# Weight splits of the second layer kept in order, a second copy of the mask, and four value cells moved

## The chip, the cores and the metric

The kernel runs on one core of one Trainium2 chip. The metric is the device time of one execution in microseconds, and the time given for a kernel is the median of several executions. The engines are TensorE (PE for its matmuls, PEld for its weight loads), VectorE (DVE), ScalarE (ACT), GpSimd (POOL) and SyncE (SP). Each has its own instruction queue, worked off in order. Transfers are started by an instruction on SP, ACT or POOL and run on the core's DMA engines beside the computing.

## The reference

Two layers over 2048 latent tokens of width 1024, with 256 context tokens in front. Layer 0 is a latent attention beside a gated linear attention. Layer 1, the one that changes here, is a neighbourhood attention of 16 heads of 64:

```python
def odd_mixer(h, hc, w_in, q_gain, k_gain, rpb, w_out, update_ctx):
    def heads(u):
        bsz, n, _ = u.shape
        q, k, v, z = jnp.split(u, 4, axis=-1)
        sh = lambda t: t.reshape(bsz, n, C_HEADS, C_HD)
        return rms_norm(sh(q), q_gain), rms_norm(sh(k), k_gain), sh(v), z

    q_x, k_x, v_x, z_x = heads(jnp.dot(h, w_in))
    q_c, k_c, v_c, z_c = heads(jnp.dot(hc, w_in))
    o = neighborhood_attention(q_x, k_x, v_x, k_c, v_c, rpb)
    y = jnp.dot(o.reshape(h.shape[0], h.shape[1], C_WIDTH) * jax.nn.silu(z_x), w_out)
```

`neighborhood_attention` lets each query see a window of 8 rows by 16 columns of the token grid and all context tokens; a bias table `rpb` is added to the window's scores, and what lies outside the window is masked. All is fp32.

## The kernel before, in words

Matrix products run in split precision: an operand is split into a high and a low part, and a product is three matmuls (lines 129 to 131: high by high, high by low, low by high). A weight is split so: SP loads a raw piece of 128x512 into `wraw`, ACT copies it to the high part, DVE subtracts that from the raw piece to make the low part (lines 380 to 383).

The program goes through layer 0, then the projection of layer 0 (`project`), then three stages of layer 1:

- `odd_qk`, queries and keys. The input weight has eight column blocks j of 512: 0 and 1 make queries, 2 and 3 keys, 4 and 5 values, 6 and 7 gates. A cell (t, j) is the product of token tile t (0 to 17, two of them context) with block j, 24 matmuls into a `gm` tile of PSUM. For queries and keys the cell is normed: ACT squares it, DVE sums (`oss`), POOL takes the power -1/2, and DVE multiplies into `onat` (line 1182). `fin` transposes `onat` on TensorE in a later cell (`tp`, line 1190), ACT and DVE copy the result (`oqh`, `oql`, `okt`), and SP and POOL store it (`Q1`, `K1`, `K1t`). The stage ends with the last two tiles over j = 0, 1, 2, 3 and 6; a gate cell goes through `gate` (line 1242) and is stored to `z1`.
- `odd_vz`, values (stored to `V1`, `V1c` from `ovz` tiles) and gates, woven with `maxes`, which finds a bound on each query's scores. Its zero halves `mz` are cleared by DVE at the stage's start.
- `odd_attention`, head by head: scores `st` from `q1`, `q2` and the keys (lines 1423, 1424), bias tables `tab0`, `tab1` with the mask added by POOL (line 1420), exponentials, products with the values `ov`.

A weight block has one of four places in SBUF (`OD_PLACE`), w0 to w3, so blocks 4, 5, 6 and 7 come into the places of 2, 3, 0 and 1 once those are done with. A generator per block, `od_steps`, makes the splits; `pump` (line 158) advances it at every fourth step of the cells, so the splits lie among the cells' other work on ACT and DVE. The order on each engine is set by a scheduler when the program is built, except where `issue_after` puts one instruction behind another of its engine. The loads of `odd_attention` go through `load` (line 111), which chains them on SP in the order of the code: second query piece of the first heads, keys, values, tables, context keys `kc`, first query piece, and so on, with the mask `maskk` behind them.

Of the kernel before, what the change touches and what calls it, by code (L numbers as in the profile page):

```python
# [10 lines left out]
F32 = mybir.dt.float32  # L11
F32R = mybir.dt.float32r
# [5 lines left out]
P = 128  # L18
# [70 lines left out]
class Kern:  # L89
    def __init__(self, tc, nc, ins, scr):  # L90
        self.tc, self.nc, self.i, self.scr = tc, nc, ins, scr
        self.n = 0
        self.ahead, self.calls, self.chain = [], 0, None

    def pool(self, es, name, bufs=1, space=None, **kw):
        if space is None:
# [100 lines left out]
    def rpow(self, out, in_, mul, add):  # L197

        g = self.nc.gpsimd
        g.tensor_scalar(out=out, in0=in_, scalar1=mul, scalar2=add, op0=ALU.mult, op1=ALU.add)  # L200
        shp = list(out.shape)
        g.tensor_tensor(out=out, in0=out, in1=self.mhalf[:, : shp[1]], op=ALU.pow)


    def consts(self, es):
# [803 lines left out]
    def even_mix(self, e1, win, hT):  # L1009
# [3 lines left out]
        with ExitStack() as es:  # L1013
# [57 lines left out]
            self.prep_pool(e1, "prp1", "left", 2, 3)  # L1071
            ws = [self.pool(e1, "owS", side="left", reuse_waits="tile")]

            def ahead():
# [59 lines left out]

    OD_PLACE = {2: 0, 3: 1, 0: 2, 1: 3, 4: 0, 5: 1, 6: 2, 7: 3}

    def od_steps(self, dst, j, ws):
        n = self.OD_PLACE[j]
        steps = self.split_steps(dst, j, ws[n // 2], self.i["w_od"][:, j], KD, 512, f"w{n}", 1)
        for k, _ in enumerate(steps):  # L1140
            if k % 2:
                yield

    def odd_qk(self, ws, win, hT):
        nc = self.nc
# [6 lines left out]
        with ExitStack() as es:  # L1152
# [5 lines left out]
            self.ahead += [self.od_steps(win, 0, ws), self.od_steps(win, 1, ws)]  # L1158
            pend, kt = [], {}

            def cell(t, j):
                hi, lo = hT[t]
                wh, wl = win[j]
                ps = self.tl(pp, [P, 8, 64], "gm", bufs=3)
                steps = self.mm3_steps(ps[:], (lambda k: hi[:, k, :], lambda k: lo[:, k, :]),
                                       (lambda k: wh[:, k, :], lambda k: wl[:, k, :]), range(KD))
                for n, _ in enumerate(steps):
                    if n == 5 and pend and (len(pend) > 1 or j == 6):
                        fin(*pend.pop(0))
                    yield  # L1170
                if j == 6:
                    n = self.tl(sp, [P, 512], "onat", bufs=4)
                    self.gate(n, ps[:].rearrange("p h d -> p (h d)"))
                    pend.append((t, j, n))
                    return
                sq = self.tl(sp, [P, 512], "osq")
                self.act(sq[:], ps[:].rearrange("p h d -> p (h d)"), AF.Square)
# [4 lines left out]
                nc.vector.tensor_tensor(out=n[:].rearrange("p (h d) -> p h d", h=8), in0=ps[:],  # L1182
                                        in1=ss[:].unsqueeze(2).to_broadcast([P, 8, 64]), op=ALU.mult)
                pend.append((t, j, n))

            def fin(t, j, n):
# [9 lines left out]
                self.act(hi[:], ps[:], AF.Copy, scale=qkg[:, z : z + 1])  # L1196
                j0 = (j % 2) * 4
                if z == 1:
                    nc.sync.dma_start(self.K1[j0 : j0 + 4, :, t * P : t * P + P].rearrange("j p t -> p j t"), hi[:].bitcast(F32))
                if z == 0 or t < NCT:  # L1200
                    lo = self.tl(sp, [P, 4, P], "oql", F32R)
                    nc.vector.scalar_tensor_tensor(out=lo[:], in0=ps[:], scalar=qkg[:, z : z + 1], in1=hi[:],
                                                   op0=ALU.mult, op1=ALU.subtract)
                    if z == 0:
                        for part, tt in enumerate((hi, lo)):
                            nc.sync.dma_start(self.Q1[part][j0 : j0 + 4, :, (t - NCT) * P : (t - NCT) * P + P].rearrange("j p t -> p j t"),
                                              tt[:].bitcast(F32))
                    else:
                        store_k((hi, lo), j0, t * P, P)
                    return  # L1210
                g, r0 = divmod(2 * (t - NCT), 8)
                if r0 == 0:
# [5 lines left out]
                    nc.vector.scalar_tensor_tensor(out=ol, in0=view(ps, 2)[:, :, r], scalar=qkg[:, z : z + 1],  # L1218
                                                   in1=view(hi, 2)[:, :, r], op0=ALU.mult, op1=ALU.subtract)
                if r0 == 6:  # L1220
                    store_k(kt.pop(j), j0, CTX + g * 512, 512)

            def store_k(parts, j0, o, w):

                for u, x in enumerate(parts):
                    for i in range(2):
                        nc.gpsimd.dma_start(self.K1t[j0 : j0 + 4, i, u * 64 : u * 64 + 64, o : o + w].rearrange("j d t -> d j t"),
                                            x[i * 64 : i * 64 + 64].bitcast(F32))

            nxt = {2: 4, 3: 5, 0: 6, 1: 7}  # L1230
            done = lambda j: j in nxt and self.ahead.append(self.od_steps(win, nxt[j], ws))
            cells = self.cells(list(range(NT)), (2, 3, 0, 1), lambda t, j: j > 1 or t >= NCT)[:-8]
            cells += [(t, j) for j in (0, 1, 2, 3, 6) for t in (NT - 2, NT - 1)]
            for _ in self.stream(cells, hT, cell, lambda t: self.prep(1, t, self.x1, pp, ("px", 2)), done):
                self.pump()
            while pend:
                fin(*pend.pop(0))

    def gate(self, out, in_):

# [16 lines left out]
    def odd_vz(self, ws, win, hT):  # L1257
# [3 lines left out]
        with ExitStack() as es:  # L1261
# [6 lines left out]
            def cell(t, j):  # L1268
                hi, lo = hT[t]
                wh, wl = win[j]  # L1270
                ps = self.tl(pp, [P, 512], "gm")
                yield from self.mm3_steps(ps[:], (lambda k: hi[:, k, :], lambda k: lo[:, k, :]),
                                          (lambda k: wh[:, k, :], lambda k: wl[:, k, :]), range(KD))
                n = self.tl(sp, [P, 512], "ovz", bufs=3)
                if j < 6:
                    self.act(n[:], ps[:])
                    self.store_v(t, j - 4, n)
                    return
                self.gate(n, ps[:])
                pt = self.tl(pp, [P, 4, P], "tp", bufs=1)  # L1280
                for i in range(4):
                    nc.tensor.transpose(pt[:, i, :], n[:, i * P : i * P + P], self.ident[:])
# [73 lines left out]
    def odd_attention(self, out, right, left, wout):  # L1356
# [4 lines left out]
        with ExitStack() as es:  # L1361
# [56 lines left out]
            def mask(tabs):  # L1418
                for tb in tabs:
                    nc.gpsimd.tensor_tensor(out=tb[:], in0=tb[:], in1=mk[:], op=ALU.add)  # L1420

            def scores(ps, k1, k2, q1, q2):
                nc.tensor.matmul(ps, k1, q1, start=True, stop=False)  # L1423
# [99 lines left out]
            all_k, most_k = slice(0, KD), slice(0, KD - 1)  # L1523
# [18 lines left out]
            for j in range(8):  # L1542
                OA[j] = {}, {}
                for s, (kind, n) in enumerate(steps):
                    g, c = divmod(n, 4)
                    if j < 7:
# [4 lines left out]
                        elif s == 7:  # L1551
                            Q[j + 1, 1] = query(j + 1, 1)
                        elif s == 13:
                            V[j + 1] = values(j + 1)
                            values_ctx(j + 1, V[j + 1])
                        elif s == 15:
                            kc[j + 1] = keys(j + 1, 0, CTX, kcp, "kc")
                        elif s == 10:
                            with self.tc.issue_after(self.psum.ins):
                                mask(tabs[j + 1])  # L1560
# [200 lines left out]
```

## Time and profile before

| | us |
|---|---|
| median of 3 runs | 3669.73 (3668.54 to 3671.02) |
| profiled execution | 3676.2 |
| its span, first to last instruction | 3674.1 |
| layer 0 | 0 to 1993 |
| projection of layer 0 | 1993 to 2172 |
| queries and keys, `odd_qk` | 2172 to 2626 |
| values and gates, `odd_vz` | 2626 to 3089 |
| `odd_attention` with its projection | 3089 to 3674 |

Times in the trace count from the start of the span. A line number belongs to the kernel whose trace it is. A matmul's duration overlaps the next one's, so that TensorE's rate is read from the starts. In a row of a timeline, what stands in brackets is how long the engine was idle before it and whose end it waited for.

### The profile page before, as it was taken

To read this page: it belongs to the slowest core of one execution; us is meant where nothing else is said; L and a number is where in the kernel's file an instruction comes from. 1 tells how busy PE (TensorE), PEld (TensorE's weight loads), DVE (VectorE), ACT (ScalarE), POOL (GpSimd) and SP (SyncE) were. 2 spreads that over 40 slices of the span, in tenths; PEclk is the share of its full clock that TensorE was granted. 3 is DMA by queue.
4 is the path that set the end of the run, shared out by engine and by line. 5 is a ranking of instruction groups with operands and counts; after the bars stand their busy time and mean duration, and the time that the engine had idled before them with its cause. 6 is when DMAs were issued, how large, how long until landed. Compare 5 with 4: busy or idle time off the path is not lost.

```text
span 3674.1 us, 51831 instructions
## 1 busy us (share of the span) xinstructions
PE 3565.7 (97%) x18404; PEld 2758.7 (75%) x18404; DVE 2363.0 (64%) x4860; ACT 1437.0 (39%) x2741; POOL 1205.6 (33%) x1336
## 2 busy tenths in 40 slices
PE   8999999999999999999999999999899999999998
PEld 6988998888886666655556878888688887555577
DVE  4677666888876666687664444454578784666721
ACT  5545551111125555555553124444422223555510
POOL 1433330101111212122201233333334443777743
PEclk9999999999999999999999999999999999999899
DMA  7455472222241232243622544455744447788554
GB/s 253 145 155 155 133 210 87 80 73 88 75 137 53 83 98 79 85 115 109 177 67 96 188 161 123 141 157 160 227 146 122 146 120 190 210 215 219 175 178 149
DMA packets 364372, 512.19 MB, mean 139 GB/s; under 512 B 25825, under 2 KB 243889, under 8 KB 358210
## 3 DMA queue, kind: packets, MB, share of 16 engines
q1 hardware_dynamic: 322642, 425.49, 39.8%
q0 software_dynamic: 19872, 55.92, 5.1%
q10 hardware_dynamic: 21600, 27.46, 2.1%
q8 instruction: 146, 2.39, 0.3%
q14 instruction: 112, 0.92, 0.1%
HBM read 329.38 MB, written 179.37 MB: 138 GB/s over the span
## 4 chain that ended last, share of the span: by engine, by line
PE 69%; issue 15%; POOL 5%; DVE 5%; DMA 4%; ACT 2%; SPq 0%; POOLq 0%; DVEq 0%; ACTq 0%
PE av L922 7%; PE gm L129 6%; PE gm L130 6%; PE gm L131 6%; PE st L980 4%; PE st L981 4%; PE st L982 4%; PE st L129 2%; PE st L131 2%; PE st L130 2%; PE pj L131 2%; PE pj L130 2%; PE pj L129 2%; PE o L1456 2%; DMA wraw<-w_od 1%
## 5 line engine op out<-in xcount | busy, mean ns | idle before, releaser
L971 DVE TENSOR_TENSOR acc<-acc,apt 128x512 f32<-128x512 f32 x512 | 364.8, 737 | 153.5 <-ACT apt L106 150.6
L106 ACT ACTIVATE apt<-st 128x512 f32<-128x512 f32 (+1 forms) x592 | 344.6, 594 | 290.5 <-PE st L982 257.4
L662 DVE TENSOR_REDUCE mm<-mx 128x1 f32<-128x512 f32 (+1 forms) x656 | 393.2, 630 | 89.9 <-PE mx L661 81.8
L922 PE MATMUL av<-apt,av 128*64 128x512 f32 (+1 forms) x1184 | 286.4, 599 | 0.0
L980 PE MATMUL st<-aq,akh 97*128 97x512 f32 (+1 forms) x592 | 255.7, 432 | 9.7 <-DMA aq<-QT 6.1
L661 PE MATMUL mx<-mk,mq 96*128 96x512 f32 (+1 forms) x656 | 238.6, 372 | 0.0
L981 PE MATMUL st<-aq,akh 96*128 96x512 f32 (+1 forms) x592 | 236.7, 400 | 0.0
L982 PE MATMUL st<-aq,akl 96*128 96x512 f32 (+1 forms) x592 | 235.3, 398 | 0.0
L1330 DVE CUSTOM_DVE_ANT_1 mx<-mx,mtab 128x217 f32<-128x217 f32 (+11 forms) x576 | 184.6, 338 | 49.2 <-PE mx L1324 37.9
L106 ACT ACTIVATE opt<-opt 128x930 f32<-128x930 f32 (+9 forms) x144 | 119.2, 830 | 248.0 <-POOL opt L1627 141.0
L106 ACT ACTIVATE u<-gm 128x352 f32<-128x352 f32 (+1 forms) x144 | 70.5, 496 | 360.4 <-PE gm L131 208.7
L1587 DVE TENSOR_TENSOR opt<-st,tab 128x64 f32<-128x64 f32 (+10 forms) x576 | 142.8, 316 | 88.2 <-PE st L1424 58.1
L922 PEld LDWEIGHTS av<-apt,av 128*64 128x64 f32 x1184 | 81.9, 138 | 156.4 <-issue 154.8
L980 PEld LDWEIGHTS st<-aq,akh 97*128 97x128 f32 x592 | 113.5, 192 | 101.6 <-issue 49.5
L1462 POOL TENSOR_TENSOR oacc<-oacc,opt 128x682 f32<-128x682 f32 (+10 forms) x144 | 169.8, 1199 | 26.4 <-ACT opt L106 25.1
L982 PEld LDWEIGHTS st<-aq,akl 96*128 96x128 f32 x592 | 114.6, 194 | 25.8
L661 PEld LDWEIGHTS mx<-mk,mq 96*128 96x128 f32 x656 | 122.7, 188 | 11.7
L981 PEld LDWEIGHTS st<-aq,akh 96*128 96x128 f32 x592 | 115.3, 195 | 18.3
L1423 PE MATMUL st<-q,kt 128*128 128x480 f32 (+5 forms) x256 | 99.6, 391 | 23.8 <-DVE opt L1587 18.9
L106 ACT ACTIVATE x<-px,modB,modA 128x128 f32<-128x128 f32 x272 | 99.3, 469 | 58.1 <-PE px L331 46.3
L129 PE MATMUL gm<-w0h,hhi 128*128 128x512 f32 x288 | 116.1, 403 | 0.0
L129 PE MATMUL gm<-w1h,hhi 128*128 128x512 f32 x288 | 115.7, 402 | 0.0
(570 smaller groups left out, 9928.1 us busy)
## 6 DMA issues: line engine op xcount, KB each, us to landing
q<-Q SPq DMA_DIRECT2D x48, 512.0 KB
H<-x ACTq DMA_DIRECT2D x36, 512.0 KB
adaw<-ada_w SPq DMA_DIRECT2D x64, 256.0 KB
x<-H SPq DMA_DIRECT2D x32, 512.0 KB
wraw<-w_od SPq DMA_DIRECT2D x64, 256.0 KB
K1t<-okt POOLq DMA_DIRECT2D x32, 512.0 KB, 7.6
kt<-K1t SPq DMA_DIRECT2D x32, 512.0 KB
mtab<-rpb_q SPq DMA_DIRECT2D x16, 899.0 KB
```

What stands on the lines that cost most here:

```text
L106: return self.nc.scalar.activation(out, in_, func, **kw)
L129: self.nc.tensor.matmul(out, lh(k), rh(k), start=j == 0, stop=False)
L130: self.nc.tensor.matmul(out, lh(k), rl(k), start=False, stop=False)
L131: yield self.nc.tensor.matmul(out, ll(k), rh(k), start=False, stop=j == n - 1)
L661: mm = nc.tensor.matmul(ps[:, :w], q[:A_QK, (t % 6) * P : (t % 6) * P + P], k[:A_QK, k0 : k0 + w], start=True, stop=True)
L662: nc.vector.tensor_reduce(out=m[:, t, n : n + 1], in_=ps[:, :w], axis=AX.X, op=ALU.max)
L922: nc.tensor.matmul(O[j, nb][i * 64 : i * 64 + 64, :w], V[j, kt // TT][:, kt % TT, i * 64 : i * 64 + 64], pts[i][:, :w], start=n == 0, stop ...
L971: nc.vector.tensor_tensor(out=acc[i][:, :w], in0=a[:, :w], in1=pts[i][:, :w], op=ALU.add)
L980: nc.tensor.matmul(ps[:, :w], kh[: A_QK + 1, i, kq], qh[: A_QK + 1, :w], start=True, stop=False)
L981: nc.tensor.matmul(ps[:, :w], kh[:A_QK, i, kq], ql[:A_QK, :w], start=False, stop=False)
L982: mm = nc.tensor.matmul(ps[:, :w], kl[:A_QK, i, kq], qh[:A_QK, :w], start=False, stop=True)
L1330: nc.vector.tensor_tensor_reduce(out=s, in0=s, in1=tb[:, ri : ri + rn, ci : ci + cn], scale=1.0, scalar=-3e38, op0=ALU.add, op1=ALU.max, a ...
```

## The change

Five things are changed.

1. `od_steps` makes one stream of all blocks that are to be split (`todo`). The low part is eight tiles of 128x512 instead of one, and the raw piece k is loaded straight into the slot of low tile k + 1; only the last goes through `wraw`, which has two buffers instead of three. Up to four pieces are loaded ahead of their splits in the order of the code.
2. `marks`: in `pump`, the splits are put behind the last cell's square, gate or copy on ACT, and behind its `onat` multiply on DVE.
3. The stores of `K1t` on POOL are issued one at a time, at the second and sixth step of a cell, behind the last power on POOL.
4. The cells (16, 4) and (17, 4), values of the last two tiles, are done at the end of `odd_qk` instead of at the start of `odd_vz`.
5. The mask is loaded twice: a first copy into a free buffer of `q10` directly behind the first heads' tables, for these tables, and a second into `maskk` as before, for the later heads.

```diff
@@ pump
-            if next(self.ahead[0], self) is not self:
+            with ExitStack() as es:
+                for x in self.marks.values():
+                    es.enter_context(self.tc.issue_after(x.ins))
+                r = next(self.ahead[0], self)
+            if r is not self:
                 break
@@ even_mix
-            self.prep_pool(e1, "prp1", "left", 2, 3)
...
-                for j in (2, 3):
-                    yield from self.od_steps(win, j, ws)
+                yield from self.od_steps(win, ws)
@@ od_steps
-    def od_steps(self, dst, j, ws):
-        n = self.OD_PLACE[j]
-        steps = self.split_steps(dst, j, ws[n // 2], self.i["w_od"][:, j], KD, 512, f"w{n}", 1)
-        for k, _ in enumerate(steps):
-            if k % 2:
-                yield
+    def od_steps(self, dst, ws):
+        nc, todo, raw, k = self.nc, self.todo, [], KD
+        def split(w, parts, pool, n, k):
+            hi, lo = parts
+            lo.append(self.tl(pool, [P, 512], f"w{n}l{k}", F32R, bufs=1))
+            self.act(hi[:, k, :], w[:])
+            nc.vector.tensor_tensor(out=lo[k][:], in0=w[:], in1=hi[:, k, :], op=ALU.subtract)
+        while raw or todo or k < KD:
+            for i in range(2):
+                if raw and (len(raw) >= 4 or k == KD and not todo):
+                    split(*raw.pop(0))
+                if k == KD and todo:
+                    j, k = todo.pop(0), 0
+                    n = self.OD_PLACE[j]
+                    pool = ws[n // 2]
+                    dst[j] = self.tl(pool, [P, KD, 512], f"w{n}h", F32R, bufs=1), []
+                if k < KD:
+                    w = self.tl(pool, [P, 512], f"w{n}l{k + 1}", bufs=1) if k < KD - 1 else self.tl(self.prp, [P, 512], "wraw", bufs=2)
+                    nc.sync.dma_start(w[:], self.i["w_od"][:, j, k])
+                    raw.append((w, dst[j], pool, n, k))
+                    k += 1
+            yield
@@ odd_qk
-                    if n == 5 and pend and (len(pend) > 1 or j == 6):
+                    if n == 5 and pend and (len(pend) > 1 or j in (4, 6)):
                         fin(*pend.pop(0))
+                    if n % 4 == 1 and out_k:
+                        with self.tc.issue_after(self.power.ins):
+                            out_k.pop(0)()
                     yield
+                if j == 4:
+                    n = self.tl(sp, [P, 512], "onat", bufs=4)
+                    self.act(n[:], ps[:].rearrange("p h d -> p (h d)"))
+                    self.store_v(t, 0, n)
+                    return
...
-            cells += [(t, j) for j in (0, 1, 2, 3, 6) for t in (NT - 2, NT - 1)]
+            cells += [(t, j) for j in (0, 1, 2, 3, 6, 4) for t in (NT - 2, NT - 1)]
@@ odd_vz
-            cells = [(t, j) for j in (7, 4, 5) for t in (NT - 1, NT - 2)]
+            cells = [(t, j) for j in (7, 5) for t in (NT - 1, NT - 2)]
@@ odd_attention
             tabs[0] = tables(0)
+            first = self.tl(qa, [P, SEQ], "q10", bufs=2)[:, : NR * NC]
+            mask(tabs[0], load_mask(first.rearrange("p (r c) -> p r c", r=NR)))
             kc[0] = keys(0, 0, CTX, kcp, "kc")
...
-            mk = self.tl(ap, [P, NR, NC], "maskk", bufs=1)
-            self.load(mk[:], self.i["maskk"].rearrange("p (r c) -> p r c", r=NR))
-            mask(tabs[0])
+            mk = load_mask(self.tl(ap, [P, NR, NC], "maskk", bufs=1)[:])
```

What this does to the order is shown at three places: first before, then after. At the start of `odd_qk`, SP loads the raw pieces of blocks 0 and 1, places w2 and w3, among the stores of keys:

```order
L380 DMA wraw_4095_19415<-w_od 128x512
L380 DMA wraw_4096_19419<-w_od 128x512
L380 DMA wraw_4107_19476<-w_od 128x512
L1199 DMA K1<-oqh_4093_19400 128x4x128
L380 DMA wraw_4108_19480<-w_od 128x512
L380 DMA wraw_4112_19510<-w_od 128x512
L380 DMA wraw_4113_19514<-w_od 128x512
L380 DMA wraw_4604_22647<-w_od 128x512
L1199 DMA K1<-oqh_4110_19495 128x4x128
```

The same place on SP after the change:

```order
L1163 DMA w3l3_4114_19428<-w_od 128x512
L1163 DMA w3l4_4116_19433<-w_od 128x512
L1163 DMA w3l5_4128_19491<-w_od 128x512
L1163 DMA w3l6_4130_19496<-w_od 128x512
L1163 DMA w3l7_4135_19527<-w_od 128x512
L1238 DMA K1<-oqh_4111_19410 128x4x128
L1163 DMA wraw_4652_22767<-w_od 128x512
L1238 DMA K1<-oqh_4132_19509 128x4x128
```

The pieces come ahead of the first store of keys, each into a slot of its own. At the end of `odd_qk`, DVE's queue before holds the splits of block 5 (`w1l`), then the copies of the last key tile (`okt`), then the multiply of the last key cell, `onat_4670`:

```order
L1179 TENSOR_REDUCE oss_4669_22998<-osq_4668_22996 128x8
L1218 SCALAR_TENSOR_TENSOR okt21_4537_22236<-tp_4664_22966,oqkg_4068_19263,oqh_4665_22971 128x256
L383 TENSOR_TENSOR w1l_4673_23018<-wraw_4674_23019,w1h_4672_23017 128x512
L383 TENSOR_TENSOR w1l_4673_23018<-wraw_4675_23023,w1h_4672_23017 128x512
L383 TENSOR_TENSOR w1l_4673_23018<-wraw_4678_23051,w1h_4672_23017 128x512
L1218 SCALAR_TENSOR_TENSOR okt31_4545_22283<-tp_4676_23033,oqkg_4068_19263,oqh_4677_23038 128x256
L383 TENSOR_TENSOR w1l_4673_23018<-wraw_4679_23055,w1h_4672_23017 128x512
L1218 SCALAR_TENSOR_TENSOR okt31_4545_22283<-tp_4676_23033,oqkg_4068_19263,oqh_4677_23038 128x256
L1182 TENSOR_TENSOR onat_4670_23002<-gm_4661_22939,oss_4669_22998 128x512
L1242 SCALAR_TENSOR_TENSOR onat_4680_23059<-onat_4680_23059,gm_4671_23004 128x512
```

DVE's queue after, where `onat_4715` is the same multiply:

```order
L1218 TENSOR_REDUCE oss_4714_23032<-osq_4713_23030 128x8
L1150 TENSOR_TENSOR w0l2_4709_23020<-w0l3_4696_22957,w0h_4689_22922 128x512
L1150 TENSOR_TENSOR w0l3_4711_23025<-w0l4_4698_22962,w0h_4689_22922 128x512
L1258 SCALAR_TENSOR_TENSOR okt21_4565_22264<-tp_4707_23001,oqkg_4082_19277,oqh_4708_23006 128x256
L1221 TENSOR_TENSOR onat_4715_23036<-gm_4702_22972,oss_4714_23032 128x512
L1150 TENSOR_TENSOR w0l4_4717_23052<-w0l5_4704_22988,w0h_4689_22922 128x512
L1150 TENSOR_TENSOR w0l5_4720_23058<-w0l6_4706_22993,w0h_4689_22922 128x512
L1258 SCALAR_TENSOR_TENSOR okt31_4573_22311<-tp_4722_23069,oqkg_4082_19277,oqh_4723_23074 128x256
L1150 TENSOR_TENSOR w0l6_4724_23088<-w0l7_4710_23023,w0h_4689_22922 128x512
L1287 SCALAR_TENSOR_TENSOR onat_4728_23098<-onat_4728_23098,gm_4716_23038 128x512
L1150 TENSOR_TENSOR w0l7_4726_23093<-wraw_4712_23028,w0h_4689_22922 128x512
L1150 TENSOR_TENSOR w1l0_4730_23115<-w1l1_4719_23056,w1h_4718_23055 128x512
```

The multiply stands ahead of all splits of block 5, which have moved behind the gate cells, and only splits of block 4 (w0) are left around it. Where attention begins, SP's chain of loads before is:

```order
L111 DMA tab0_5482_27513<-rpb_k 128x1034
L111 DMA tab1_5483_27514<-rpb_k 128x1034
L111 DMA kc1_5484_27517<-K1t 128x2x256
L111 DMA kc20_5474_27494<-K1t 64x2x256
L111 DMA q10_5485_27520<-Q1 64x2048 x2
L111 DMA q20_5486_27521<-Q1 64x2048
L111 DMA q20_5486_27521<-M1 1x2048
L111 DMA kt1_5487_27526<-K1t 128x2x512
L111 DMA kt21_5477_27497<-K1t 64x2x512
L111 DMA ov_5481_27511<-V1c 128x2x128
L111 DMA maskk_5488_27530<-maskk 128x1034
```

And after:

```order
L111 DMA tab0_5538_27569<-rpb_k 128x1034
L111 DMA tab1_5539_27570<-rpb_k 128x1034
L111 DMA q10_5540_27573<-maskk 128x1034
L111 DMA kc1_5541_27577<-K1t 128x2x256
L111 DMA kc20_5530_27550<-K1t 64x2x256
L111 DMA q10_5542_27580<-Q1 64x2048 x2
L111 DMA q20_5543_27581<-Q1 64x2048
L111 DMA q20_5543_27581<-M1 1x2048
L111 DMA kt1_5544_27586<-K1t 128x2x512
L111 DMA kt21_5533_27553<-K1t 64x2x512
L111 DMA ov_5537_27567<-V1c 128x2x128
L111 DMA maskk_5545_27590<-maskk 128x1034
```

The mask's first copy, in a `q10` buffer, has come in behind the tables; the rest follows as before. The buffers' places in SBUF have moved as well: with `wraw` one buffer smaller, `tab1` of the first heads takes up a stretch that the last `ovz` tile of `odd_vz` occupied, and its load waits in the program for that tile's store to `V1c` and for ACT's copy into it. Before, this was not so for any load ahead of the second heads' tables.

More of the change, by code (lines that the diff above doesn't have):

```diff
@@ L92, in __init__ @@
         self.n = 0
-        self.ahead, self.calls, self.chain = [], 0, None
+        self.ahead, self.calls, self.chain, self.marks = [], 0, None, {}
     def pool(self, es, name, bufs=1, space=None, **kw):
@@ L201, in rpow @@
         shp = list(out.shape)
-        g.tensor_tensor(out=out, in0=out, in1=self.mhalf[:, : shp[1]], op=ALU.pow)
+        self.power = g.tensor_tensor(out=out, in0=out, in1=self.mhalf[:, : shp[1]], op=ALU.pow)
     def consts(self, es):
@@ L1208, in fin @@
                     else:
-                        store_k((hi, lo), j0, t * P, P)
+                        for f in store_k((hi, lo), j0, t * P, P):
+                            f()
                     return
@@ L1220, in fin, with store @@
                 if r0 == 6:
-                    store_k(kt.pop(j), j0, CTX + g * 512, 512)
+                    out_k.extend(store_k(kt.pop(j), j0, CTX + g * 512, 512))
             def store_k(parts, j0, o, w):
[L1225 to L1228, printed above, removed]
+                def store(u, x, i):
+                    nc.gpsimd.dma_start(self.K1t[j0 : j0 + 4, i, u * 64 : u * 64 + 64, o : o + w].rearrange("j d t -> d j t"),
+                                        x[i * 64 : i * 64 + 64].bitcast(F32))
+                return [lambda u=u, x=x, i=i: store(u, x, i) for u, x in enumerate(parts) for i in range(2)]
             nxt = {2: 4, 3: 5, 0: 6, 1: 7}
-            done = lambda j: j in nxt and self.ahead.append(self.od_steps(win, nxt[j], ws))
+            done = lambda j: j in nxt and self.od_ahead(win, ws, nxt[j])
             cells = self.cells(list(range(NT)), (2, 3, 0, 1), lambda t, j: j > 1 or t >= NCT)[:-8]
-            cells += [(t, j) for j in (0, 1, 2, 3, 6) for t in (NT - 2, NT - 1)]
+            cells += [(t, j) for j in (0, 1, 2, 3, 6, 4) for t in (NT - 2, NT - 1)]
             for _ in self.stream(cells, hT, cell, lambda t: self.prep(1, t, self.x1, pp, ("px", 2)), done):
@@ L1237, in odd_qk @@
                 fin(*pend.pop(0))
+            for f in out_k:
+                f()
+            self.marks = {}
     def gate(self, out, in_):
@@ L1416, in tables, with mask, load_mask @@
                 return tabs
-            def mask(tabs):
+            def mask(tabs, mk):
                 for tb in tabs:
-                    nc.gpsimd.tensor_tensor(out=tb[:], in0=tb[:], in1=mk[:], op=ALU.add)
+                    nc.gpsimd.tensor_tensor(out=tb[:], in0=tb[:], in1=mk, op=ALU.add)
+            def load_mask(mk):
+                self.load(mk, self.i["maskk"].rearrange("p (r c) -> p r c", r=NR))
+                return mk
             def scores(ps, k1, k2, q1, q2):
```

24 lines of the change are left out of this document (15 added, 9 removed).

## The prediction

> **What bounds the kernel now.** I read the page's busy times first, then busy time by stage, then the waits of TensorE in the stages that the change touches, then the two timelines where a wait is long.
>
> ```profile
> PE 3565.7 (97%) x18404; PEld 2758.7 (75%) x18404; DVE 2363.0 (64%) x4860; ACT 1437.0 (39%) x2741; POOL 1205.6 (33%) x1336
> ...
> 1993.00:2172.00 179.00, 177.63 (x787) 146.08 (x786) 70.16 (x75) 32.24 (x50) 45.46 (x36) 1.00 0.55 178
> 2172.00:2626.50 454.50, 438.14 (x2097) 361.10 (x2096) 236.74 (x368) 217.12 (x413) 173.95 (x219) 0.98 0.54 161
> 2626.50:3089.00 462.50, 457.45 (x2227) 382.79 (x2226) 328.31 (x1361) 116.20 (x193) 188.45 (x168) 0.99 0.48 146
> 3089.00:3130.00 41.00, 36.36 (x218) 23.23 (x218) 21.96 (x65) 18.92 (x30) 28.30 (x22) 0.92 0.83 212
> ```
>
> A stage row holds its stretch, its length, busy time of PE, PEld, DVE, ACT and POOL, the granted clock, the DMA share and GB/s. TensorE is the bound. No matmul is added or removed (the four value cells only change stage), so only TensorE's idle time and slowed time can move: 454.50 - 438.14 = 16.4 us idle in queries and keys, 5.0 in values and gates, 4.6 at the start of attention. The waits name them (us in total, times, longest), those of queries and keys first:
>
> ```profile
> PE tp L1190 <- DVE onat L1182: 8.4, 3, 6.7
> PE tp L1190 <- ACT oqh L106: 3.0, 1, 3.0
> PE px L331 <- DVE x L328: 2.9, 1, 2.9
> PE gm L129 <- DVE hhi L343: 1.9, 1, 1.9
> ...
> PE tp L1282 <- DVE ovz L1242: 5.0, 2, 3.1
> PE st L1423 <- DVE opt L1587: 4.2, 2, 3.6
> ```
>
> Idle time is followed by slowed matmuls. In these stretches PE is busy but for the second, and the granted clock (third figure from the end) is half:
>
> ```profile
> 2199.80:2203.20 3.40, 3.31 (x10) 2.71 (x11) 3.15 (x6) 2.33 (x6) 1.35 (x4) 0.50 1.00 318
> 2617.00:2626.50 9.50, 6.28 (x20) 4.79 (x20) 5.60 (x9) 5.78 (x11) 3.67 (x6) 0.50 0.73 199
> 2640.20:2643.60 3.40, 3.40 (x10) 2.63 (x9) 0.00 (x0) 0.70 (x2) 2.40 (x1) 0.51 1.05 394
> 2817.70:2821.10 3.40, 3.40 (x11) 2.91 (x11) 3.37 (x14) 0.51 (x1) 0.00 (x0) 0.51 0.49 188
> 3099.50:3104.40 4.90, 4.90 (x14) 2.42 (x16) 2.90 (x17) 2.77 (x4) 3.18 (x3) 0.50 0.78 238
> ```
>
> Half the busy time is lost there: 1.7, 3.1, 1.7, 1.7 and 2.4 us.
>
> **The end of queries and keys (splits kept in order, value cells as filler).** ACT and DVE in order of time:
>
> ```profile
> 2614.22 0.63 ACT L106 ACTIVATE w1h<-wraw 128x512 fp32r<-128x512 f32 x1 [4.20 <-DMA wraw<-w_od]
> ...
> 2614.88 0.69 DVE L383 TENSOR_TENSOR w1l<-wraw,w1h 128x512 fp32r<-128x512 f32 x1 [4.15 <-ACT w1h L106]
> 2616.00 0.68 DVE L1182 TENSOR_TENSOR onat<-gm,oss 128x512 f32<-128x512 f32 x1
> 2629.89 0.48 DVE L1291 MEMSET mz<- 64x512 f32 x1 [4.67 <-DMA z<-oqh]
> 2637.16 1.03 DVE L1291 MEMSET mz<- 64x512 f32 x2 [6.79 <-DMA z<-oqh]
> ```
>
> The reader is to see a queue: a split whose raw piece has not landed stops ACT, its other half stops DVE, and the `onat` multiply behind it makes TensorE wait 6.7 us. Afterwards DVE waits for the gate store `z<-oqh` before it clears `mz`, so that the `ovz` multiply behind that clearing comes 3.1 us late. The change puts `onat` ahead of the w1 splits and two more cells in front of the stores' readers. A matmul starts every 0.23 us, so a cell of 24 takes 5.5 us (rows of the junction, below). What can go is 8.4 - 0.9 (one of the three waits is at the stage's start) + 3.0 + 3.1 = 13.6 us, with 3.1 + 1.7 of clock: 18.4. I take 15, since the splits, the loads of `maskq`, `mk` and `mq`, and the gate stores still have to land in time in the longer tail.
>
> **The start of queries and keys.** The 2.9 us wait and the 0.9 us behind it come from the same kind of queue:
>
> ```profile
> 2195.93 1.29 DVE L383 TENSOR_TENSOR w3l<-wraw,w3h 128x512 fp32r<-128x512 f32 x2 [2.55 <-ACT w3h L106]
> 2197.14 0.75 DVE L328 TENSOR_SCALAR x<-x,ssx 128x1024 f32<-128x1024 f32 x1
> ```
>
> With raw pieces loaded into eight slots of the weight itself instead of three shared ones, the loads run ahead. 2.9 + 0.9 + 1.7 of clock = 5.5 us; I take 4, since sixteen 256 KB loads then also run against the tiles' own loads.
>
> **Smaller terms.** The 1.9 us wait for `hhi`: 1 us taken. The second `tp <- ovz` wait, 5.0 - 3.1 = 1.9 us with 1.7 of clock at 2817, lies in a stage whose order shifts without a reason to mend it: 0, between -3.6 and +3.6. In the projection 179.00 - 177.63 = 1.4 us is idle: half taken, 0.7. The spread stores of K1t go behind POOL's `pow`; an issue takes some 0.6 us of POOL (four in 2.48 us), but the buffers they read come free later, and they are issued between cells that need `oss`. The row nearest to that is the 3.0 us wait for `oqh`: -2.5 taken, with nothing and -5 as ends. Gains so far 15 + 4 + 1 + 0.7 - 2.5 = 18.2 us.
>
> ```profile
> 2623.64 2.48 POOL L1227 DMA_DIRECT2D K1t<-okt  x4 [0.33 <-ACT okt L106]
> ```
>
> **The junction to attention.** Here the change costs. The last matmuls of values and gates, the last store, and SP's loads (start, us of issue, what):
>
> ```profile
> 3088.27 0.39 PE L130 MATMUL gm<-w1l,hhi 128*128 128x512 f32 x1
> 3088.50 0.39 PE L131 MATMUL gm<-w1h,hlo 128*128 128x512 f32 x1
> 3088.73 0.39 PE L1423 MATMUL st<-q,kc 128*128 128x512 f32 x1
> ...
> 3065.81 1.45 SPq L111 DMA_DIRECT2D tab<-rpb_k  x2
> 3067.35 1.03 SPq L111 DMA_DIRECT2D kc<-K1t  x2
> 3068.43 2.60 SPq L111 DMA_DIRECT2D q<-Q  x3
> ...
> 3089.82 0.54 POOL L1251 DMA_DIRECT2D V1c<-ovz  x1 [2.41 <-ACT ovz L106]
> 3094.50 4.69 POOL L1420 TENSOR_TENSOR tab<-tab,maskk 128x1034 f32<-128x1034 f32 x2 [4.14 <-DMA maskk<-maskk]
> ...
> DMA to landing us min/median/max: 2.3/8.2/10.0
> ```
>
> Before, both tables, `kc` and `q10`/`q20` are issued 20 us ahead of the last matmul (3065.81 against 3088.5), so the scores follow on it at 3088.73; what waits later is the mask, 4.2 us. In the changed program `tab1` of the first heads lies over the buffer of the last `ovz` tile, because `wraw` is one buffer smaller and everything behind it moves down 2 KB. Its load therefore waits until the last `V1c` store has landed, and behind it in SP's queue stand the mask, `kc1`, `kc20`, both `q10`, `q20`, which the first scores read.
>
> Worked out from the last matmul's end G = 3088.9: the store is issued at G + 0.9 and lands 2.3 to 10.0 us later (last row above, of the four such stores), so `tab1` starts at G + 3.2 to G + 10.9. I take the quick end: the slow stores had maskk, q and table loads beside them, and now nothing is ahead of the wait. Sizes on the path:
>
> ```profile
> q<-Q SPq DMA_DIRECT2D x48, 512.0 KB
> tab<-rpb_k SPq DMA_DIRECT2D x16, 517.0 KB
> kc<-K1t SPq DMA_DIRECT2D x8, 256.0 KB
> kc<-K1t SPq DMA_DIRECT2D x8, 128.0 KB
> maskk<-maskk SPq DMA_DIRECT2D x1, 517.0 KB
> ...
> 3093.00:3099.50 6.50, 2.26 (x9) 1.28 (x8) 3.74 (x10) 0.44 (x1) 4.69 (x2) 0.85 0.92 229
> ```
>
> Table, mask, keys and three query pieces are 517 + 517 + 256 + 128 + 3 x 512 = 2954 KB = 3.02 MB: 13.2 us at the 229 GB/s of this stage, 7.7 us at the 394 GB/s above, the fastest stretch shown. I take 229, since its transfers are of the same kinds. Six matmuls (1.4 us) need no `q20` and run while it comes. So the scores lose 3.2 + 13.2 - 1.4 = 15.0 us, and the old wait of 4.2 falls away: net 10.8 us worse. Both quick: 5.3. Slow store: 10.9 + 13.2 - 1.4 - 4.2 = 18.5. The slowed stretch behind the stall is there before and after.
>
> [...]
>
> **Sum.** -18.2 + 10.8 = -7.4 us. The profiled execution took 3676.2 us (span 3674.1, 2.1 outside it), so 3668.8 for it. The median of the runs, 3669.73, stands 6.5 lower; the same difference gives 3662.3.
>
> Three gaps of 2.9, 3.1 and 1.9 us are each followed by a half-clock row above (2199.8, 2640.2, 2817.7). [...]
>
> **The rivals.**
> - The junction is cheap. The store lands in 2.3 us, the loads run at 394 GB/s, and the scores' first loads prove to be elsewhere than I place them, so that it costs from 0 to 5.3 us: -18.2 + 0 to 5.3, so 3651.5 to 3657. For it: SP's queue is empty but for these loads. Against it: `q` rows are long pieces on 64 partitions, in the 229 GB/s stage.
> - The junction is dear. The last store lands after 10.0 us, as the slowest did: -18.2 + 18.5 = +0.3, 3670. For it: the median landing, 8.2 us, is nearer to this end. Against it: a busier DMA then.
> - Slower: the wait at the end of queries and keys moves and does not go. The w1 splits still stand in ACT's queue ahead of the copy of the last gate tile and of the values; eight pieces of 256 KB, 2.1 MB, must land within the two cells (11 us) before they are due, 191 GB/s. Below that rate ACT stops again, the gate store leaves late, and `mz`, `ovz` and TensorE with it. The stage had 199 GB/s in the slowed stretch, so it is close. Then the 15 us are not won: +7.6, and with another 4.2 us of ACT's waiting +11.8: 3677 to 3681.5.
>
> **How the numbers follow.** 0.2% is 7.3 us, about what a measurement of this kernel can tell from no change. My forecast, 0.43, has 3656 to 3668 as its own range and its middle on that border: 0.23 faster, 0.20 same. Cheap junction 0.19, all faster. Dear junction 0.13, same. The moved wait 0.25, slower. So faster 0.42, same 0.33, slower 0.25. The range leaves a tenth out on each side: the cheap end, 3651.5, less the 3.6 us of the 2817 term gives 3648; above, the moved wait's 3681.5, taken to 3682.
>
> **What the changed profile would show.** Right: no `tp <- onat` wait over 1 us, no `px <- x` wait at the stage's start; SP's `tab1` issued some 3 us behind the last `gm` matmul, TensorE idle 12 to 16 us before the first `st`, and no wait for a mask afterwards. Wrong, if `tab1` is issued before the last matmul, if ACT or DVE still stand at a split for microseconds, or if the first transposes of values and gates wait for `mz`.

## The result and the profile after

The changed kernel takes 3670.12 us (median), the kernel before 3669.64 us on the same chips: a ratio of 1.000, with a 95% interval of 0.9992 to 1.0008. Nothing is won or lost that a measurement can tell. Inside, much has moved. First busy time by stage of the kernel before, cut at the last transposes of queries and keys and at the last `gm` matmul (stretch, length, then PE, PEld, DVE, ACT, POOL, granted clock, DMA share, GB/s):

```profile
0.00:1994.10 1994.10, 1944.29 (x10102) 1498.17 (x10102) 1410.83 (x2272) 841.78 (x1732) 421.53 (x608) 0.98 0.39 114
2172.00:2623.00 451.00, 434.64 (x2089) 358.28 (x2088) 234.66 (x365) 215.75 (x411) 170.78 (x214) 0.98 0.54 161
2623.00:3088.90 465.90, 460.85 (x2235) 385.55 (x2234) 330.38 (x1365) 117.49 (x195) 191.62 (x173) 0.99 0.48 146
3088.90:3129.90 41.00, 36.36 (x218) 23.20 (x219) 21.86 (x65) 18.89 (x30) 28.20 (x22) 0.92 0.83 211
3129.90:3674.10 544.20, 513.02 (x2988) 347.99 (x2983) 295.47 (x722) 210.81 (x325) 347.98 (x285) 0.97 0.68 190
```

The same cuts in the changed kernel:

```profile
0.00:1986.50 1986.50, 1936.97 (x10102) 1490.81 (x10102) 1409.77 (x2272) 841.23 (x1732) 424.50 (x608) 0.99 0.38 115
2164.40:2613.00 448.60, 444.17 (x2132) 366.32 (x2130) 236.49 (x367) 216.48 (x413) 174.53 (x220) 0.99 0.56 164
2613.00:3069.70 456.70, 450.30 (x2193) 375.75 (x2191) 334.17 (x1362) 115.67 (x192) 188.29 (x166) 0.99 0.45 140
3069.70:3110.70 41.00, 25.00 (x122) 16.14 (x122) 14.60 (x38) 12.89 (x20) 14.76 (x10) 0.75 0.94 237
3110.70:3664.80 554.10, 521.00 (x3080) 354.30 (x3080) 302.07 (x747) 217.28 (x334) 361.94 (x297) 0.98 0.67 192
```

The spans differ by 9.3 us, but 7.6 of that is layer 0, whose code and order are the same in both: 1994.1 against 1986.5 at a granted clock of 0.98 against 0.99. TensorE's busy time there, for the same matmuls, makes 7.3 of the 7.6 (1944.29 against 1936.97). So these two executions are compared from layer 1 on. Queries, keys, values and gates together went from 451.0 + 465.9 = 916.9 to 448.6 + 456.7 = 905.3 us, 11.6 less. From the last `gm` matmul to the end it went from 585.2 to 595.1, 9.9 more. The sum is -1.7, and the medians, 0.5 apart, cannot tell it from nothing.

The waits of TensorE from the projection to the first heads, in the changed kernel (us in total, times, longest):

```profile
PE st L1472 <- DMA q<-Q: 14.9, 1, 14.9
PE gm L129 <- DVE hhi L347: 4.2, 2, 2.3
PE mx L1369 <- DVE mm L1364: 2.2, 2, 2.0
PE tp L1327 <- DVE ovz L1287: 1.7, 1, 1.7
PE st L1472 <- DVE opt L1636: 1.3, 3, 0.7
PE mx L1369 <- DVE mm L1375: 1.2, 1, 1.2
PE mx L1362 <- ACT mz L106: 1.2, 1, 1.2
```

The waits for `onat` and `oqh` are gone, and so is the 3.1 us wait for `ovz` at the start of values and gates; that for the tile's `x` is down to 0.2 us. In their place stand short ones of the bounds (`mx`) and one for `hhi`, and one of 14.9 us in front of the first scores. Around that one, TensorE's timeline:

```profile
3069.31 0.40 PE L131 MATMUL gm<-w1h,hlo 128*128 128x512 f32 x1
3084.62 1.62 PE L1472 MATMUL st<-q,kc 128*128 128x512 f32 x3 [14.91 <-DMA q<-Q]
```

And those of POOL, ACT and SP:

```profile
3070.64 0.54 POOL L1296 DMA_DIRECT2D V1c<-ovz  x1 [4.96 <-ACT ovz L106]
3058.53 0.37 ACTq L1331 DMA_DIRECT2D z<-ozt  x1
3064.64 8.77 SPq L111 DMA_DIRECT2D tab<-rpb_k  x2
3073.50 0.38 SPq L111 DMA_DIRECT2D q<-maskk  x1
3075.19 1.87 SPq L111 DMA_DIRECT2D q<-Q  x3
```

The last store goes out at 3070.64, the second table's issue ends at 3073.4 (3064.64 + 8.77), the mask follows, and the queries arrive at 3084.6. But the reader should also see that the first table is issued only at 3064.64, 5 us before the last matmul; before the change it was 23 us.

### The profile page after: what moved, and what is told of

It is laid out like the page before. It is cut to its first block, busy times and chain, and to the rows that moved or that the text cites. A ratio compares the mean times of both kernels' runs of the same rounds, so it can differ in the third digit from the quotient of the medians.

```text
span 3664.8 us, 51824 instructions
## 1 busy us (share of the span) xinstructions
PE 3554.0 (97%) x18404; PEld 2748.8 (75%) x18404; DVE 2368.9 (65%) x4860; ACT 1435.1 (39%) x2741; POOL 1210.8 (33%) x1336
## 5 line engine op out<-in xcount | busy, mean ns | idle before, releaser
L1375 DVE CUSTOM_DVE_ANT_1 mx<-mx,mtab 128x465 f32<-128x465 f32 (+14 forms) x576 | 184.1, 338 | 48.9 <-PE mx L1369 33.7
L986 PEld LDWEIGHTS st<-aq,akl 96*128 96x128 f32 x592 | 114.2, 193 | 25.7
L985 PEld LDWEIGHTS st<-aq,akh 96*128 96x128 f32 x592 | 114.7, 194 | 18.2
```

The costliest lines, as they stand in the source:

```text
L985: nc.tensor.matmul(ps[:, :w], kh[:A_QK, i, kq], ql[:A_QK, :w], start=False, stop=False)
L986: mm = nc.tensor.matmul(ps[:, :w], kl[:A_QK, i, kq], qh[:A_QK, :w], start=False, stop=True)
L1375: nc.vector.tensor_tensor_reduce(out=s, in0=s, in1=tb[:, ri : ri + rn, ci : ci + cn], scale=1.0, scalar=-3e38, op0=ALU.add, op1=ALU.max, a ...
```

## The experiments

Each is compared with the kernel before on the same chip; e1 to e4 ran on one chip, f1 to g1 on a second, h1 to h3 and e5 on a third, so that between these groups the ratios are compared. "The stall" is TensorE's wait before the first scores.

**The place of tab1.**

```diff
-self.tl(self.prp, [P, 512], "wraw", bufs=2)
+self.tl(self.prp, [P, 512], "wraw", bufs=3)
```

> The changed kernel with three wraw buffers again instead of two, so that the first heads' tab1 no longer lies over the last ovz tile; nothing else is touched. Theory (the buffer's place makes the stall): tab1 is issued before the last gm matmul, the 14.9 us of idle time in front of the first scores go, and part of the slowed stretch behind them with it: 10 to 15 us less than the changed kernel, 3655 to 3660 us. Rival (the additional mask load in the queue makes keys and queries late wherever tab1 lies): a wait of 8 us or more stays in front of the first scores, 3667 to 3671 us.

Measured: 3669.29 us, ratio 0.9994 (0.9985 to 1.0003). The timelines of TensorE and SP in e1, with the first load of attention in front:

```profile
3082.78 1.62 PE L1472 MATMUL st<-q,kc 128*128 128x512 f32 x3 [9.58 <-DMA q<-Q]
...
3047.46 1.72 SPq L111 DMA_DIRECT2D q<-Q  x3
3068.89 0.83 SPq L111 DMA_DIRECT2D tab<-rpb_k  x2
```

What SP waited for in e1 over these stages (us in total, times, longest):

```profile
SPq L111 <- PE mx L1369: 17.6, 1, 17.6
SPq L111 <- DMA z<-ozt: 17.2, 2, 10.8
```

Both tables now go out at 3068.89, ahead of the last matmul, as the theory had it. But the stall only falls from 14.9 to 9.6 us, and the time hardly moves: the rival's wait of 8 us or more. So `tab1`'s buffer was the wait that ended last, and another stood behind it. SP's waits name it: a landing of `z<-ozt`, a gate store with which the tables share no data. In the program it is a completion counter that is handed round: each load or store of SP and ACT takes the next of eight, and waits until its previous user has landed. In the changed order `tab0` came to follow the last gate store; in the kernel before, SP's waits of these stages name no gate store. The mask's additional load, which the rival named as the cause, is not it: e2 below has no such load there, and its stall is 10.0 us.

**The counter.**

```diff
-                nc.scalar.dma_start(self.z1[...], z[:])
+                (nc.gpsimd if t == NCT else nc.scalar).dma_start(self.z1[...], z[:])
```

> As e1_three_wraw, and the two gate stores of the last latent tile go out from POOL instead of ACT. Nothing that the tables read or write is touched by that. In e1_three_wraw the load of tab0 was issued at 3068.89, when the last gate store, issued by ACT at 3062.68, had landed; in the program it waits for that store's completion counter, which the two share only because the counters are handed round. Theory (that shared counter is the second half of the stall): tab0 is issued 15 us or more before the last gm matmul, TensorE waits under 2 us before the first scores, 9 to 14 us less than e1_three_wraw: 3655 to 3661 us. Rival (the loads from tab0 to q20 are held by something else, the last gate cell's matmuls or the DMA engines): a wait of 5 us or more stays and the time is within 5 us of e1_three_wraw.

> The changed kernel with its two wraw buffers, and the two gate stores of the last latent tile from POOL. Theory (two waits in series, tab0 for the gate store and tab1 for the last V1c store, of which the second ends later): tab0 goes out early, tab1 still some 3 us behind the last gm matmul, and TensorE idles 12 to 15 us before the first scores; 3667 to 3672 us. Rival (only the gate store counted, and the place of tab1 is harmless once tab0 is early): under 4 us of idle time there, 3656 to 3662 us.

Measured: f1 3665.33 us, 0.9981 (0.9971 to 0.9991), stall 6.1 us. f2 3674.95 us, 1.0010 (1.0001 to 1.0019), stall 15.1 us. The timelines of TensorE and SP in f1:

```profile
3082.18 1.62 PE L1472 MATMUL st<-q,kc 128*128 128x512 f32 x3 [6.14 <-DMA q<-Q]
3054.63 10.16 SPq L111 DMA_DIRECT2D tab<-rpb_k  x1
```

TensorE's wait and SP's timeline in f2:

```profile
PE st L1472 <- DMA q<-Q: 15.1, 1, 15.1
...
3051.79 25.25 SPq L111 DMA_DIRECT2D tab<-rpb_k  x2
```

f2 bears out the series: with the counter free, `tab1` still holds the queue for the rest of 25 us and the stall is as long as ever. f1 bears it out in part. The issue of `tab0` begins 21 us before the last matmul (3075.64), yet 6.1 us of stall stay: that is what the rival had forecast, and both the theory (under 2) and the price on it were off. The issue of `tab0` alone took SP 10 us, with the queries, keys and 1 MB of values of the same heads just ahead. The DMA engines had no time to spare during it (the last figure but one is their share):

```profile
3054.60:3064.80 10.20, 10.20 (x49) 8.30 (x48) 1.15 (x2) 3.02 (x5) 4.20 (x7) 1.00 1.06 247
```

From there to the first scores the share is 1.05 as well. So what f1 lacks is time for the loads: from the first of them (3050.30) to the first scores (3082.18) they take 31.9 us, and the last matmul ends 25.7 us behind their start.

**What the moved cells covered.** The first load of attention, `q11`, waits for the last matmul of the bounds (the 17.6 us row above). From there 160 `gm` matmuls followed in the kernel before, and 108 in the changed one: two cells have left the stage, and the bounds are woven in at a fixed rate from its start. 52 matmuls at 0.23 us are 11.9 us less time for the loads. Two kernels test it, one that puts the cells back and one that weaves the bounds faster:

```diff
-cells += [(t, j) for j in (0, 1, 2, 3, 6, 4) for t in (NT - 2, NT - 1)]
+cells += [(t, j) for j in (0, 1, 2, 3, 6) for t in (NT - 2, NT - 1)]
...
-cells = [(t, j) for j in (7, 5) for t in (NT - 1, NT - 2)]
+cells = [(t, j) for j in (7, 4, 5) for t in (NT - 1, NT - 2)]
```

> As e1_three_wraw, and with the value cells of the last two tiles back at the start of values and gates. Theory (these cells cover the landing of the gate stores that the clearing of mz waits for): the transposes of ovz wait again for some 3 us with a slowed stretch, 3 to 6 us slower than e1_three_wraw. Rival (the order of the splits alone removed that wait, and the stores of the moved cells are what mz waits for now): the same or up to 4 us faster.

```diff
-self.weave(gemms, maxes(), 0.57, 15)
+self.weave(gemms, maxes(), 0.59, 15)
```

> As e1_three_wraw, with the bounds of the queries woven at 0.59 instead of 0.57 into the cells of values and gates. In the program 160 gm matmuls followed the last mx matmul before the change, 108 do in the changed kernel and in e1_three_wraw, since two cells have left the stage; at 0.59 they are 159. The first load of attention waits for that mx matmul. Theory (the moved cells took 52 matmuls, 11.9 us, from the time in which attention's loads run): the wait before the first scores, 9.6 us in e1_three_wraw, falls below 1.5 us, and the time by 8 to 12 us: 3657 to 3661 us. Rival (the bounds then run against DVE, and what is won at the junction is lost at mx and ovz in the stage; or the tables still wait for the last gate store): within 4 us of e1_three_wraw.

Measured: e3 3660.62 us, 0.9970 (0.9958 to 0.9981). h1 3648.6 us, 0.9930 (0.9916 to 0.9945). Waits of TensorE in e3, and SP's issue of the first load of attention:

```profile
PE tp L1229 <- ACT oqh L106: 5.4, 1, 5.4
PE tp L1327 <- DVE ovz L1287: 1.3, 1, 1.3
PE tp L1229 <- DVE okt L1258: 1.1, 1, 1.1
...
3039.43 1.73 SPq L111 DMA_DIRECT2D q<-Q  x3
```

In h1, TensorE at the end of the stage, then SP's issue of that load and of the tables:

```profile
3068.05 0.40 PE L131 MATMUL gm<-w1h,hlo 128*128 128x512 f32 x1
3068.28 0.39 PE L1472 MATMUL st<-q,kc 128*128 128x512 f32 x1
...
3031.07 1.73 SPq L111 DMA_DIRECT2D q<-Q  x3
3044.01 2.03 SPq L111 DMA_DIRECT2D tab<-rpb_k  x2
```

The same load in the kernel before, whose first scores start at 3088.73:

```profile
3051.25 1.73 SPq L111 DMA_DIRECT2D q<-Q  x3
```

In e3 and h1 TensorE no longer waits for the loads of the first scores; in h1 they start 0.23 us after the last `gm` matmul. `q11` goes out 37.2 us ahead of them in h1 (3031.07 against 3068.28), 37.5 ahead in the kernel before, and in e1 only 25.7 ahead of the last `gm` matmul's end (3082.78 less 9.58 of stall is 3073.2, less 3047.46). The tables' issue is at 3044, 24 us ahead, and SP's waits in h1 name no gate store, so the counter does not matter either. e3 shows what the cells are worth where they went: without them 5.4 + 1.1 us of waiting for `oqh` and `okt` come back at the end of queries and keys, more than the 3 us for `ovz` that I had expected, which is 1.3. Yet the time, where I had expected 3 to 6 us more, is 9 us below e1: the cells cost more at the junction than they bring. h1 keeps both, and gains more than the 8 to 12 us expected. It lies 20.7 us below e1 in the medians (of two chips), and the traces of the two differ by 15.1 us from layer 1 on. Of these 9.6 are the stall, and the rest is of the size of what the clock takes behind it, which I had not priced. TensorE's half-clock stretch after the start of the scores, first in e1, then in h1:

```profile
3082.80:3098.20 15.40, 14.75 (x38) 10.02 (x40) 8.97 (x28) 7.34 (x12) 3.21 (x3) 0.50 1.03 237
...
3078.20:3081.60 3.40, 3.40 (x10) 0.97 (x8) 0.89 (x7) 1.32 (x2) 3.24 (x3) 0.50 0.99 306
```

Half the busy time is lost in each, 7.4 us in e1 and 1.7 in h1. Worked out in the same way for the 45 us behind the last `gm` matmul, the eight traces with a stall lose 4.6 to 9.0 us, the five without one and with the early mask 1.7 each. So a stall here cost some 3 to 7 us more than its length. The 5.6 us between medians and traces are not placed: they are within what layer 0 alone differed by above.

**The mask.** e2 is e1 with one copy, loaded late as before; g1 is the kernel before with the early copy alone.

```diff
-            first = self.tl(qa, [P, SEQ], "q10", bufs=2)[:, : NR * NC]
-            mask(tabs[0], load_mask(first.rearrange("p (r c) -> p r c", r=NR)))
...
             mk = load_mask(self.tl(ap, [P, NR, NC], "maskk", bufs=1)[:])
+            mask(tabs[0], mk)
```

> As e1_three_wraw, and with one copy of the mask only, loaded behind the values as before the change. Theory (the mask was late by its place in the queue): the wait of the scores for the masked table comes back, some 4.2 us with its slowed stretch, so 3 to 7 us slower than e1_three_wraw. Rival (with the stall before it gone or moved the mask is in time anyway): within 2 us of e1_three_wraw.

> The kernel before with the mask's second copy alone, loaded behind the first tables into a q10 buffer. Theory (the mask was late by its place in the queue): the 4.2 us in which the scores waited for the masked table go with part of the slowed stretch behind them, 3662 to 3667 us. Rival (the load takes the place of keys and queries behind it, which then are late by as much): 3668 to 3673 us.

Measured: e2 3670.61 us, 0.9997 (0.9988 to 1.0007); g1 3667.36 us, 0.9996 (0.9987 to 1.0005). By the times neither can be told from its base, which for e2 is what the rival said. The traces can. TensorE's wait for the masked table in e2:

```profile
PE st L1472 <- DVE opt L1635: 4.1, 3, 3.2
```

In e1, with the early copy:

```profile
PE st L1472 <- DVE opt L1636: 0.8, 3, 0.3
```

And in g1:

```profile
PE st L1427 <- DVE opt L1591: 2.4, 4, 1.1
```

With the mask late the wait is 4.1 us, with it early 0.8; with the early copy in the kernel before it falls from 4.5 (longest 3.6) to 2.4, in pieces of at most 1.1. The mechanism holds and is worth some 2 to 3 us of waiting, less than the 4.2 that I had set. Not every wait for `opt` is the mask's: in h1, where the mask is in place before the first scores, six short ones of at most 1.1 us still make 3.9.

**The marks.** e4 is e1, f3 is f1, h2 is h1 and h3 is e3, each with the splits no longer put behind the cells' own work:

```diff
-                for x in self.marks.values():
+                for x in ():
```

> As e1_three_wraw, with the splits no longer put behind the last cell's square, copy and multiply; the raw pieces still come early into the slots of the low parts. Theory (what stood in the way was a split in front of the cell's own work): waits of TensorE for onat come back in queries and keys, 5 to 12 us in all. Rival (the splits only hurt because their pieces were late, and early loads cure that by themselves): within 2 us of e1_three_wraw.

> As f1_three_wraw_gate_pool, with the splits no longer put behind the last cell's work. Theory (from e4_three_wraw_no_marks, 5.5 us below e1_three_wraw: with early pieces the splits do not hold up the cells, and being put behind them only makes splits late): 2 to 6 us less than f1_three_wraw_gate_pool. Rival (that difference was scatter between executions): within 2 us of it.

> As h1_three_wraw_ratio59, with the splits no longer put behind the last cell's work. Theory (from e4 and f3, 5.5 and 1.5 us below the same kernels with marks, and 3.1 and 1.7 us shorter up to the last gm matmul): 1 to 4 us less than h1_three_wraw_ratio59. Rival (marks make no difference once pieces come early): within 1 us of it.

> As e3_three_wraw_no_fill, with the splits no longer put behind the last cell's work. Theory (without the two extra cells the splits of block 5 fall into the tail of queries and keys, where only the marks keep them behind the last key tile): waits for onat of 3 to 7 us come back there, 3 to 8 us more than e3_three_wraw_no_fill. Rival (early pieces alone do it, as with the extra cells): within 2 us of it or less.

Measured: e4 3663.75 us, 0.9983 (0.9974 to 0.9992), f3 3663.8 us, 0.9984 (0.9973 to 0.9994), h2 3642.11 us, 0.9920 (0.9904 to 0.9936), h3 3658.47 us, 0.9959 (0.9946 to 0.9971). No pair is apart by more than its intervals, so that neither the gains expected for f3 and h2 nor the loss expected for h3 is shown by the times. In the traces e4, f3 and h2 reach their last `gm` matmul 3.0, 1.7 and 4.7 us sooner in layer 1 than their twins with marks, h3 3.4 us later. Waits of TensorE in h2:

```profile
PE gm L129 <- DVE hhi L347: 3.5, 2, 1.9
PE tp L1229 <- DVE onat L1221: 0.9, 1, 0.9
```

And in h3:

```profile
PE tp L1229 <- ACT oqh L106: 7.0, 1, 7.0
PE tp L1229 <- DVE onat L1221: 0.9, 1, 0.9
```

So my theory for e4, that waits for `onat` of 5 to 12 us come back, is wrong: 0.9 us does. Early pieces in slots of their own are, by elimination, what cured the queue (no kernel here goes without them alone); putting the splits behind the cells adds nothing once the two cells stand at the end, and seems to cost a little. Without those cells (h3) the wait for `oqh` grows from 5.4 to 7.0 and the stages are longer, which the time does not show.

**The spread stores.**

```diff
-out_k.extend(store_k(kt.pop(j), j0, CTX + g * 512, 512))
+[f() for f in store_k(kt.pop(j), j0, CTX + g * 512, 512)]
```

> As e1_three_wraw, with the four stores of a K1t group issued together again. Theory (my price for the spread stores, 2.5 us of waits for the buffers that they read): 1 to 4 us less than e1_three_wraw. Rival (POOL's issues never reach TensorE's path): within 2 us of it, with the same waits in queries and keys.

Measured: 3665.94 us, 0.9992 (0.9980 to 1.0003), against 0.9994 for e1. Queries to gates take 903.9 us in its trace and 904.3 in that of e1. The rival: these stores are not on TensorE's path either way.

The best of these, h2, is the change with the three `wraw` buffers, bounds woven at 0.59 and no marks: 29.8 us below the kernel before by the medians (3642.11 against 3671.91).

## Why the prediction was right, and where not

The forecast was 3662.3 us with a chance of 0.42 for faster; the kernel is at 3670.1, in the range, which was wide, and in the class that had 0.33. The mechanisms that it named are there, and so is each sign that it gave for being right: no wait for `onat`, none over 0.2 us for `x`, `tab1` some 3 us behind the last matmul, a stall of 12 to 16 us, and no wait for a mask. What it forecast as won and lost does not come out as a gain, though. Point by point:

- The end of queries and keys: the old waits went, as forecast, 13.6 us with their slowed stretches, 18.4. What came is late next in the following stage: 1.2, 1.2 and 2.0 us at `mx` and one slowed stretch of 1.7, 6.1 in all. That leaves 12.3 for the 15 taken. My text gave the credit to `onat` being put ahead of the splits; by e4 the early pieces do it without that being forced.
- The start: the 2.9 + 0.9 us went, but `hhi` now waits 2.3 us with a slowed stretch of 1.7: 1.5 for the 4 taken. The wait for `hhi` at 2554 stayed as it was, and this time with a slowed stretch of 1.7 behind it (1 taken, -1.7 got). The second `ovz` wait fell only from 1.9 to 1.7 (0 taken), the projection kept its 1.4 (0.7 taken). The -2.5 for spread stores was nothing (e5). These pieces make 12.3 + 1.5 - 1.7 + 0.2 = 12.3; measured over the stages it is 11.6, instead of 18.2.
- The junction: 15.0 us of stall forecast, 14.9 measured, by the same steps: the issue of `tab1` starts 3.4 us behind the last matmul (3.2 forecast), the scores at 14.9. From the last `gm` matmul on, 9.9 us worse for 10.8. That these two lie so near is partly luck. By the stage rows TensorE's idle time there rose by 13.3 us, from 35.8 to 49.1, and its busy time, for the same matmuls, fell by 3.4, as half-clock stretches fell otherwise in the two executions. The prediction also put the slowed stretch behind the stall at the same before and after; it lost 2.4 us before, and 4.6 in the changed kernel (half clock from the scores at 3084.6 to 3094.1).

So the term that was mis-sized is the gain. 18.2 - 11.6 = 6.6 us are most of the 7.9 between -7.4 and the +0.5 of the medians. And one step was wrong in kind: "no matmul is added or removed (the four value cells only change stage)". They are two cells, here and in the title, and they did change more than stage: 52 matmuls of cover for attention's loads. Had `tab1` not waited, I would have forecast a junction at no cost; e1 shows that 9.6 of the 14.9 us would have stayed.

The rival with a cheap junction did not come. The dear one put the time at 3670, where it is, but for another reason: the store landed 2.2 us after its issue. The moved wait, which was to make it slower, is seen in small at `mx`; at the end of queries and keys ACT waits for no raw piece any more, where it waited 10.5 us before.

## What to carry to other kernels

A wait that ends last hides those that end just before it: undoing it alone gained 5 of 15 us here, and the profile named the next only when it was gone. A stall cost more than its length here, with the clock at half (0.50) behind it: some 3 to 7 us more. Work that is moved out of a stage to fill a gap takes with it the time in which the next stage's loads ran, so the point where those loads are released (here the last bound) has to move as well. A smaller buffer moves everything behind it: look at what comes to lie over what, and which store a load then waits for.

## What the runs showed of the hardware

The clock was not expected to differ so between executions of the same code. The same 1.87 us gap (TensorE's wait for `hhi` in the last tiles of queries and keys) was followed by full speed in the kernel before and by half in the changed one. The end of the gap and the stretch behind it in the kernel before:

```profile
2556.20 0.50 PE L129 MATMUL gm<-w2h,hhi 128*128 128x512 f32 x1 [1.87 <-DVE hhi L343]
2556.30:2559.70 3.40, 3.40 (x15) 2.80 (x16) 2.20 (x4) 0.79 (x3) 0.14 (x1) 1.00 0.61 221
```

And in the changed kernel:

```profile
2547.82 0.68 PE L129 MATMUL gm<-w2h,hhi 128*128 128x512 f32 x1 [1.87 <-DVE hhi L347]
2548.00:2551.40 3.40, 3.40 (x9) 2.64 (x10) 2.11 (x4) 0.70 (x3) 0.06 (x1) 0.50 0.59 213
```

15 matmuls fit into 3.4 us in the one and 9 in the other. In the clock records of these two traces the clock is full or half (1.00 or 0.50), and each half-clock stretch but the one in which a trace ends is 3.41 us long or a whole multiple of that: 22 such stretches before and 16 after, from 3.41 to 20.48 us. So the same gap cost 1.9 us in the one execution and 3.6 in the other (1.87, and half of the 3.4 behind it). What decides between the two is not shown. A gain read from one execution of each kernel can be off by several microseconds: layer 0 alone differed by 7.6.

The other surprise is the issue of one load: 10.16 us on SP for `tab0` in f1, where it takes 0.83 for two in e1. In f1 the DMA share is 1.06 during it; in e1 it is 0.78 in the 13 us before. That a full DMA is what holds the issue up is suggested by these rows, not shown.
